# Two gate/up groups per FFN as seven block products instead of eight, in a two-layer decoder trunk on one core

## The chip, the cores and the metric

One NeuronCore of a Trainium2 chip runs the whole kernel in one launch. The metric is the device time of an execution in microseconds (us). TensorE (PE in the profile) multiplies, VectorE (DVE) and ScalarE (ACT) work elementwise, GpSimd (POOL) takes small tasks, SyncE (SP) issues DMAs.

## The reference, cut to what matters

Two layers on 256 tokens of width 1024, in float32. Each layer is FFN, mixer, FFN; four FFNs in all, with an inner width of 2816 = 5 x 512 + 256. Layer 0 mixes by causal pooling, layer 1 by dilated window attention whose keys and values come from the residual stream after layer 0.

```python
def swiglu(h, w_gate, w_up, w_down):
    return (jax.nn.silu(h @ w_gate) * (h @ w_up)) @ w_down

def reference(...):
    for layer in range(DEPTH):
        g = norm_gain[layer]
        f = swiglu(rms_norm(h, g[0]), ffn_w_gate[layer, 0], ffn_w_up[layer, 0], ffn_w_down[layer, 0])
        h = h + 0.5 * rms_norm(f, g[1])
        hm = rms_norm(h, g[2])
        mix = pool_mixer(hm, ...) if layer < N_A_LAYERS else dilated_mixer(hm, ...)
        h = h + rms_norm(mix, g[3])
        f = swiglu(rms_norm(h, g[4]), ffn_w_gate[layer, 1], ffn_w_up[layer, 1], ffn_w_down[layer, 1])
        h = h + 0.5 * rms_norm(f, g[5])
        if layer == N_A_LAYERS - 1:
            k_sh, v_sh = shared_kv(h, kv_norm_gain, w_k, w_v, cos, sin)
    return h
```

## The kernel before

**Precision by parts.** Every float32 operand is split in two float32r parts: `hi`, a cast, and `lo`, the rest. A product is three matmuls: hi·hi, hi·lo, lo·hi. For a weight unit (a tile of 128 x 1024) the load comes from one packed stream `ws`, ScalarE casts (line 92) and VectorE subtracts (line 93); `load_unit` does all three. The raw tile has four buffers (`rawp`), the parts eight (`hlp`, tag `hl`).

**Work order of an FFN.** The normed activations lie transposed in `aT` (two token halves of 128, eight blocks of 128 of the inner dimension). The gate and up columns are taken in five groups of 512 and a last one of 2 x 256. A group of gate, or of up, is four units; `both` goes through them and multiplies each for both token halves, 2 x 2 x 3 = 12 matmuls of 512 columns a unit. `gate` applies SiLU on ScalarE, `up` multiplies on VectorE, `turn` transposes the product on TensorE (four 128 x 128 blocks) and splits it into parts in `h2`. `turn` for group c runs inside the gate half of group c + 1. Gate results lie in the two PSUM banks of `gup`, up results in the four of `accp`. Then 22 units of the down weights follow, one for each block of 128 rows, each with 12 matmuls; the last six (`TAIL`) are first used for token half 0, then for half 1, so that the norms of half 0 run beside matmuls. `Bound` is what lies between two stages: `post` (norm and residual), `norm` (the next stage's), `transposed` (TensorE transposes into PSUM, cast and subtraction into `aT`).

**Order.** The tile framework orders VectorE, ScalarE and TensorE in the FFNs ahead of time by its own planned times, with program order as the priority, and then puts in the waits; on the chip each engine goes through its list in order. In the attention stage the order of TensorE, VectorE and ScalarE is that of the program (`manual_schedule`). SP issues the loads in order, and each waits until its raw buffer is free.

**Other places that the change touches.** `kv_input` norms and transposes the stream for keys and values; it runs in FFN 2 after group 2 (`middle`). In attention `next_q` loads one unit of query weights at a time, `q_turn` copies the transposed queries out of PSUM (line 611), `p_turn` and `values` handle the probabilities, and `o_proj` multiplies by the output weights.

Of the kernel before, what the change touches and what calls it, by code (L numbers as in the profile page):

```python
# [26 lines left out]
NG = 5  # L27
TAIL = 6
WARM = 64
CAST = 1024  # L30
# [17 lines left out]
def trunk_kernel(ctx: ExitStack, tc: tile.TileContext, x, pos, gains, pscale, ws, wq, invf, amask, pmat, icnt, out):  # L48
# [6 lines left out]
    s8p = ctx.enter_context(tc.tile_pool(name="s8p", bufs=6))  # L55
# [25 lines left out]
    unit_no = [0]  # L81
    last = {}

    def load_unit():
        u = unit_no[0]
        unit_no[0] += 1
        raw = rawp.tile([P, 1024], F32, tag="raw", name=f"raw{u}")
        last["dma"] = nc.sync.dma_start(raw, ws[u])
        hl = hlp.tile([P, 2, 1024], F32R, tag="hl", name=f"hl{u}")
        for c in range(0, 1024, CAST):  # L90
            w = slice(c, c + CAST)
            nc.scalar.copy(hl[:, 0, w], raw[:, w])  # L92
            last["dve"] = nc.vector.tensor_sub(hl[:, 1, w], raw[:, w], hl[:, 0, w])  # L93
        return hl

    def load_q_unit(u):
        raw = rawp.tile([P, 1024], F32, tag="raw", name=f"rawq{u}")
        nc.sync.dma_start(raw[:, :768], wq[u])
        hl = hlp.tile([P, 2, 1024], F32R, tag="hl", name=f"hlq{u}")
        nc.scalar.copy(hl[:, 0, :768], raw[:, :768])  # L100
        nc.vector.tensor_sub(hl[:, 1, :768], raw[:, :768], hl[:, 0, :768])  # L101
        return hl
# [4 lines left out]
    def proj_mm(o, aT, i, units, n, nk=8, only=None):  # L107

        per = nk // len(units)
        for q, u in enumerate(units):  # L110
            if only is not None and q != only:
                continue
            for k in range(per):
                kc = q * per + k
                lo, hi = k * n, (k + 1) * n
                t = slice(i * P, (i + 1) * P)
                mm(o, aT[:, 0, kc, t], u[:, 0, lo:hi], kc == 0, False)
                mm(o, aT[:, 0, kc, t], u[:, 1, lo:hi], False, False)
                mm(o, aT[:, 1, kc, t], u[:, 0, lo:hi], False, kc == nk - 1)

    def row_mm(f, l_hi, l_lo, u, first, last):

        mm(f[0], l_hi, u[:, 0, 0:512], first, False)
        mm(f[1], l_hi, u[:, 0, 512:1024], first, False)
        mm(f[0], l_hi, u[:, 1, 0:512], False, False)
        mm(f[1], l_hi, u[:, 1, 512:1024], False, False)
        mm(f[0], l_lo, u[:, 0, 0:512], False, last)
        mm(f[1], l_lo, u[:, 0, 512:1024], False, last)

    def half_mm(f, k, l_hi, l_lo, u, first, last):  # L130
        n = slice(k * 512, (k + 1) * 512)
        mm(f[k], l_hi, u[:, 0, n], first, False)
        mm(f[k], l_hi, u[:, 1, n], False, False)
        mm(f[k], l_lo, u[:, 0, n], False, last)
# [40 lines left out]
    def transposed(i, src, dst, name):  # L175

        for b in range(2):
# [6 lines left out]
            nc.vector.tensor_sub(d[:, 1], tp, d[:, 0])  # L184

# [25 lines left out]
    def ffn(n, aT, boundary, middle=None):  # L211

        h2 = [s8p.tile([P, 2, 4, S], F32R, tag="s8", name=f"h2_{n}_{c}") for c in range(NG + 1)]
        act, prod = {}, {}

        def gate(c, i, g):
            w = g.shape[-1]
            act[c, i] = sc2.tile([P, 512], F32, tag="w2", name=f"s_{n}_{c}{i}")
            nc.scalar.activation(act[c, i][:, :w], g, AF.Silu)

        def up(c, i, u):
            w = u.shape[-1]
            prod[c, i] = sc2.tile([P, 512], F32, tag="w2", name=f"m_{n}_{c}{i}")
# [11 lines left out]
        def both(ps, units, c=None):  # L235

            for q in range(4):
                for i in range(2):
                    proj_mm(ps[i], aT, i, units, 512, only=q)
                if c is not None and q < 2:  # L240
                    turn(c, q)

        units = [load_unit() for _ in range(8 - len(first_units))]
        units, first_units[:] = first_units + units, []
# [11 lines left out]
        for c in range(1, NG):  # L256
            units = [load_unit() for _ in range(4)]
            ps = [gup.tile([P, 512], F32, tag="gu", name=f"g_{n}_{c}{i}") for i in range(2)]
            both(ps, units, c - 1)
            for i in range(2):  # L260
                gate(c, i, ps[i])
            units = [load_unit() for _ in range(4)]
            ps = acc_pair(f"u{n}{c}")
            both(ps, units)
            for i in range(2):
                up(c, i, ps[i])
            if c == 2 and middle is not None:
                middle()
        units = [load_unit() for _ in range(4)]
        ps = [gup.tile([P, 512], F32, tag="gu", name=f"g_{n}_{NG}{i}") for i in range(2)]  # L270
        both(ps, units, NG - 1)
        for i in range(2):
            gate(NG, i, ps[i][:, 0:256])
            up(NG, i, ps[i][:, 256:512])

# [7 lines left out]
        for c in range(NF - TAIL):  # L283
            u = load_unit()
            down(c, 0, u)
            down(c, 1, u)
            if c < 2:
                turn(NG, c, 2)
        tail = [load_unit() for _ in range(TAIL)]
# [12 lines left out]
    class Bound:  # L302


        def __init__(self, n, post_idx, half, pre_idx):
            self.n, self.half, self.idx = n, half, (post_idx, pre_idx)

        def prepare(self):
            self.gpost = load_gain(self.idx[0], "post")
            self.gpre = load_gain(self.idx[1], "pre")  # L310
            self.aT = new_aT(self.n)

# [6 lines left out]
        def third(self, i):  # L319
            transposed(i, self.y, self.aT, self.n)  # L320
# [7 lines left out]
    aT = new_aT("x")  # L328
    with tc.manual_schedule(engines={mybir.EngineType.DVE, mybir.EngineType.Activation}):
        y = norm(0, gpre, "x")  # L330
        first_units += [load_unit()]
# [457 lines left out]
```

## Time and profile before

| | before |
|---|---|
| median of 3 runs | 991.42 us (991.13 to 992.21) |
| profiled execution | 991.82 us, span 990.0 us |
| mean granted TensorE clock | 0.992 |
| PE busy | 966.5 us, 98% |
| DVE busy | 577.4 us, 58% |
| ACT busy | 482.8 us, 49% |
| POOL busy | 55.0 us, 6% |
| DMA read | 178.54 MB |

The span runs from the first to the last instruction of the profiled execution. "Busy" is the time in which an engine works; matmuls are pipelined, so their spacing says more than the duration of one. A row of the groups gives line, engine, operation, result and operands, shapes and count, then the busy time in us and the mean of one in ns, then the idle time just before and what ended it. A row of the chain gives start, duration and what ran. A row of a timeline ends in brackets with the idle time before it and what released it. A row of the stretches gives the bounds, the length, and for PE, weight loads, DVE, ACT and POOL the busy time and count, then the granted clock, the DMA share and GB/s.

### The profile page before, as it was taken

How to read it: one execution, taken by the hardware profiler on the slowest of the kernel's cores; microseconds unless marked ns; L12 is line 12 of the kernel's file. 1: busy time of each engine (PE TensorE's matmuls, PEld its weight loads, DVE VectorE, ACT ScalarE, POOL GpSimd, SP SyncE). 2: the span in 40 equal slices, each digit the busy share in tenths (PEclk: the TensorE clock that was granted, in tenths of full speed). 3: DMA queues.
4: the chain of work that ended last, by engine and by line, in shares of the span. 5: the costliest groups of instructions: out<-in, count | busy, mean ns of one | idle time of the engine just before them, and what ended most of it. 6: DMA issues, size and time to landing. Idle time of an engine off the chain costs nothing.

```text
span 990.0 us, 12277 instructions
## 1 busy us (share of the span) xinstructions
PE 966.5 (98%) x4656; PEld 798.4 (81%) x4656; DVE 577.4 (58%) x740; ACT 482.8 (49%) x665; POOL 55.0 (6%) x50
## 2 busy tenths in 40 slices
PE   7999999999999999999999999999999999999997
PEld 6888888878788888887888888788878678888886
DVE  5665554578765555447666554695366856555542
ACT  5644443366554444347554443554355755444431
POOL 0000000010100000001000000100033500000000
PEclk8999999999999999999999999999999989999999
DMA  6855655656465565535855655475233527556531
GB/s 234 296 178 185 229 187 186 206 192 214 148 214 190 183 229 183 191 128 168 275 181 174 227 187 192 149 234 177 90 98 116 174 83 255 190 190 200 185 128 42
DMA packets 53723, 180.39 MB, mean 182 GB/s; under 512 B 7264, under 2 KB 7264, under 8 KB 53664
## 3 DMA queue, kind: packets, MB, share of 16 engines
q1 hardware_dynamic: 53584, 179.35, 54.9%
q8 instruction: 36, 0.59, 0.2%
q0 software_dynamic: 80, 0.26, 0.1%
q14 instruction: 23, 0.19, 0.1%
HBM read 178.54 MB, written 1.05 MB: 181 GB/s over the span
## 4 chain that ended last, share of the span: by engine, by line
PE 82%; DVE 6%; ACT 4%; issue 4%; POOL 2%; DMA 1%; SPq 0%; POOLq 0%; DVEq 0%; ACTq 0%
PE g L105 22%; PE acc_d L105 21%; PE acc_u L105 19%; PE acc_b L105 7%; PE vp L105 3%; PE kp L105 3%; PE htp L230 2%; DVE hl L93 2%; PE acc_w L105 1%; DVE h L171 1%; PE qp L105 1%; ACT hl L92 1%; ACT p L554 1%; POOL rs_qf L156 1%; DMA gain_pre<-in_gains 1%
## 5 line engine op out<-in xcount | busy, mean ns | idle before, releaser
L93 DVE TENSOR_TENSOR hl<-raw,hl 128x1024 fp32r<-128x1024 f32 x310 | 379.4, 1226 | 295.7 <-ACT hl L92 293.3
L92 ACT CAST hl<-raw 128x1024 fp32r<-128x1024 f32 x310 | 325.2, 1051 | 330.9 <-PE acc_d L105 100.6
L105 PE MATMUL acc_d<-hl,h 128*128 128x512 f32 x1056 | 242.9, 390 | 0.0
L105 PEld LDWEIGHTS acc_d<-hl,h 128*128 128x128 f32 x1056 | 197.4, 188 | 40.6
L105 PE MATMUL g<-hl,aT_m 128*128 128x512 f32 x480 | 116.2, 394 | 0.0
L105 PEld LDWEIGHTS g<-hl,aT_m 128*128 128x128 f32 x480 | 88.6, 188 | 18.0
L105 PE MATMUL acc_u<-hl,aT_m 128*128 128x512 f32 x384 | 88.3, 389 | 0.0
L105 PEld LDWEIGHTS acc_u<-hl,aT_m 128*128 128x128 f32 x384 | 72.1, 188 | 15.0
L105 PE MATMUL acc_u<-hl,aT_f 128*128 128x512 f32 x288 | 67.2, 390 | 0.0
L105 PEld LDWEIGHTS acc_u<-hl,aT_f 128*128 128x128 f32 x288 | 53.8, 188 | 11.4 <-DVE aT_f L184 0.5
L105 PE MATMUL g<-hl,aT_f 128*128 128x512 f32 x240 | 58.8, 396 | 0.0
L105 PE MATMUL g<-hl,aT_x 128*128 128x512 f32 x240 | 58.1, 394 | 0.0
L105 PEld LDWEIGHTS g<-hl,aT_x 128*128 128x128 f32 x240 | 44.3, 188 | 9.0
L105 PEld LDWEIGHTS g<-hl,aT_f 128*128 128x128 f32 x240 | 44.2, 188 | 8.8
L105 PE MATMUL acc_b<-hl,aT_m 128*128 128x512 f32 x192 | 47.5, 408 | 1.2 <-ACT aT_m L183 1.1
L105 PEld LDWEIGHTS acc_b<-hl,aT_m 128*128 128x128 f32 x192 | 37.7, 198 | 9.9 <-ACT aT_m L183 1.3
L105 PE MATMUL acc_u<-hl,aT_x 128*128 128x512 f32 x192 | 44.2, 389 | 0.0
L105 PEld LDWEIGHTS acc_u<-hl,aT_x 128*128 128x128 f32 x192 | 36.0, 188 | 7.5
L105 PE MATMUL qp<-hlq,aT_f 128*128 128x384 f32 x192 | 38.1, 345 | 1.2 <-DVE hlq L101 1.1
L561 POOL TENSOR_SCALAR p<-p,rd 128x512 f32<-128x512 f32 x16 | 30.3, 1905 | 105.8 <-DVE rd L560 99.5
L105 PEld LDWEIGHTS qp<-hlq,aT_f 128*128 128x128 f32 x192 | 32.8, 188 | 3.4 <-DVE hlq L101 2.0
L105 PE MATMUL kp<-hl,aT_hk 128*128 128x512 f32 x144 | 34.6, 394 | 0.0
(156 smaller groups left out, 835.3 us busy)
## 6 DMA issues: line engine op xcount, KB each, us to landing
raw<-in_ws SPq DMA_DIRECT2D x310, 512.0 KB, 3.4
rawq<-in_wq SPq DMA_DIRECT2D x16, 384.0 KB, 3.2
gain_post<-in_gains SPq DMA_DIRECT2D x14, 256.0 KB, 4.9
gain_pre<-in_gains SPq DMA_DIRECT2D x12, 256.0 KB, 5.9
rawpm<-in_pmat SPq DMA_DIRECT2D x2, 512.0 KB, 5.0
out_dram<-h SPq DMA_DIRECT2D x4, 256.0 KB, 2.1
h<-in_x SPq DMA_DIRECT2D x2, 256.0 KB, 3.1
h<-in_x SPq DMA_DIRECT2D x1, 512.0 KB, 8.4
```

The lines of the kernel that those rows point to most:

```text
L92: nc.scalar.copy(hl[:, 0, w], raw[:, w])
L93: last["dve"] = nc.vector.tensor_sub(hl[:, 1, w], raw[:, w], hl[:, 0, w])
L105: nc.tensor.matmul(o, l, r, start=start, stop=stop)
L156: nc.gpsimd.tensor_tensor(rs, ms, nhalf, op=ALU.pow)
L171: nc.vector.scalar_tensor_tensor(h[i][:, c], y[:, c], rs, h[i][:, c], op0=ALU.mult, op1=ALU.add)
L230: nc.tensor.transpose(tp[:, k], prod[c, i][:, k * P : (k + 1) * P], ident)
L554: nc.scalar.activation(p, p, AF.Exp, bias=nm, scale=0.125, accum_out=den)
L561: nc.gpsimd.tensor_scalar_mul(p, p, rd)
```

## The change

Groups 1 and 3 of each FFN are computed with seven block products instead of eight (Winograd's form of Strassen's scheme). The blocks are two token halves by two halves of the inner dimension for the activations, and two halves of the inner dimension by gate and up columns for the weights: x and w are the gate's two halves, y and z the up's. The products are A00·x, A01·w, S0·(x+y), S1·(x+y+z), S3·z, S2·(y+z) and A11·(x+y+z+w), all weight sums formed in place and S0 to S3 are sums of activation blocks, made by the new class `Sums` out of the transposes' PSUM tiles. Results are put together in PSUM by accumulating into the same bank, and by additions on VectorE (c01, c11, p1). Group c + 1 of a pair stays plain, its matmuls set between the products.

Two of a pair's four weight sums are VectorE additions (k = 0, 1), two are accumulating DMAs issued from GpSimd (k = 2, 3, `DMA_SUMS`). The weight stream is laid out in blocks of 128 x 2048, loaded as two DMAs into one raw tile; `form` casts and subtracts a whole block at once into two parts buffers. Raw tiles have three buffers of twice the size, parts six; two more buffers (`xyp`) hold x and y of a pair, and the parts of the first units of some plain groups. The sums of activations take a place in the pool of `aT`, so `kv_input` moves from the middle of FFN 2 to after its last gate/up group (`late`). In attention, query weights are loaded two units at a time, the queries are copied out in three pieces, three buffers instead of four hold the transposed probabilities, and the last output products are set otherwise between the other steps.

```diff
-    rawp = ctx.enter_context(tc.tile_pool(name="rawp", bufs=4))
-    hlp = ctx.enter_context(tc.tile_pool(name="hlp", bufs=8))
+    rawp = ctx.enter_context(tc.tile_pool(name="rawp", bufs=3))
+    xyp = ctx.enter_context(tc.tile_pool(name="xyp", bufs=2))
+    hlp = ctx.enter_context(tc.tile_pool(name="hlp", bufs=6))
...
+    def form(raw):
+
+        hi, lo = [hlp.tile([P, 2, 1024], F32R, tag="hl", name=f"hl_{z}") for z in ("hi", "lo")]
+        nc.scalar.copy(hi, raw)
+        last["dve"] = nc.vector.tensor_sub(lo, raw, hi)
+        return [(hi[:, k], lo[:, k]) for k in range(2)]
...
+        def add_half(self, i, b, tp):
+            a = self.a
+            if (i, b) != (1, 1):
+                a[i, b] = self.tmp(f"{i}{b}")
+                nc.scalar.copy(a[i, b], tp)
+            if (i, b) == (1, 0):
+                s3 = self.tmp("s")
+                nc.vector.tensor_sub(s3, a[0, 0], tp)
+                self.parts(2, s3)
+            if (i, b) == (1, 1):
+                nc.vector.tensor_sub(a[1, 0], tp, a[1, 0])
+                self.parts(0, a[1, 0])
+                nc.vector.scalar_tensor_tensor(a[0, 0], a[0, 0], -1.0, a[1, 0], op0=ALU.mult, op1=ALU.subtract)
+                self.parts(1, a[0, 0])
+                nc.vector.scalar_tensor_tensor(a[0, 1], a[0, 1], -1.0, a[0, 0], op0=ALU.mult, op1=ALU.subtract)
+                self.parts(3, a[0, 1])
+
+        def parts(self, k, src):
+            nc.scalar.copy(self.out[:, k, 0], src)
+            nc.vector.tensor_sub(self.out[:, k, 1], src, self.out[:, k, 0])
...
+        def add(dst, src, k):
+            if k in DMA_SUMS:
+                nc.gpsimd.dma_start(dst, src, accum_op=ALU.add)
+            else:
+                nc.vector.tensor_add(dst, dst, src)
+
+        def pair(c, turns):
+
+            g = [gup.tile([P, 512], F32, tag="gu", name=f"g_{n}_{c}{i}") for i in range(2)]
+            us = load_form()
+            both(g, us + us, (0,))
+            turns[0]()
+            both(g, us + us, (1,))
+            x, y = [load_raw(xyp, "xy") for _ in range(2)]
+            px = bank()
+            product(px, plain(0, 0), form(x), True)
+            p1 = temp("p1")
+            nc.scalar.copy(p1, px)
+            turns[1]()
+            z = load_raw()
+            add(x, y, 0)
+            py = bank()
+            product(py, summed(0), form(x), True)
+            p5 = temp("p5")
+            nc.scalar.copy(p5, py)
+            us = load_form()
+            both(g, us + us, (2, 3))
+            for i in range(2):
+                gate(c + 1, i, g[i])
+            add(x, z, 1)
+            product(px, summed(1), form(x), False)
+            u1 = temp("u1")
+            nc.scalar.copy(u1, px)
+            product(py, summed(3), form(z), False)
+            c01 = temp("c01")
+            nc.vector.scalar_tensor_tensor(c01, py, -1.0, u1, op0=ALU.mult, op1=ALU.subtract)
+            add(y, z, 2)
+            g = [gup.tile([P, 512], F32, tag="gu", name=f"u_{n}_{c}{i}") for i in range(2)]
+            us = load_form()
+            both(g, us + us, (0, 1))
+            product(px, summed(2), form(y), False)
+            c11 = temp("c11")
+            nc.vector.scalar_tensor_tensor(c11, px, -1.0, p5, op0=ALU.mult, op1=ALU.subtract)
+            w = load_raw()
+            pz = bank()
+            product(pz, plain(0, 1), form(w), True)
+            nc.vector.tensor_add(p1, pz, p1)
+            gate(c, 0, p1)
+            up(c, 0, c01)
+            add(x, w, 3)
+            product(px, plain(1, 1), form(x), False)
+            gate(c, 1, px)
+            up(c, 1, c11)
+            us = load_form()
+            both(g, us + us, (2,))
+            turn(c, 0)
+            both(g, us + us, (3,))
+            for i in range(2):
+                up(c + 1, i, g[i])
...
+        pair(1, [lambda: turn(0, 0), lambda: turn(0, 1)])
+        if middle is not None:
+            middle()
...
+        pair(3, [turns12, lambda: turn(2, 1)])
...
+        if late is not None:
+            late()
...
-        nc.scalar.copy(qT[pr // 2][:, pr % 2, :, i * P : (i + 1) * P], tp[:, :3])
+        for g in range(3):
+            nc.scalar.copy(qT[g][:, pr, i * P : (i + 1) * P], tp[:, g])
```

More of the change, by code (lines that the diff above doesn't have):

```diff
@@ L79, in trunk_kernel @@
         nc.tensor.matmul(warm[:, 0:P], zeros, zeros, start=True, stop=True)
-    unit_no = [0]
+    block_no = [0]
     last = {}
[L84 to L94, printed above, removed]
@@ new lines, in load_units, with load_form, load_q_units @@
+    def load_units(n, xy=False):
+        units = []
+        for b in range(n // 2):
+            raw = load_raw()
+            units += [parts(raw, k, xy=xy and b == 0) for k in range(2)]
+        return units
+    def load_form():
+        return form(load_raw())
+    def load_q_units(pr, b):
+        raw = rawp.tile([P, 2, 1024], F32, tag="raw", name=f"rawq{pr}{b}")
+        nc.sync.dma_start(raw[:, :, :768], wq[pr * 2 + b])
+        return [parts(raw, k, 768, pr % 2 == 0 and b == 0) for k in range(2)]
@@ L233, in turn, with both, bank @@
             nc.vector.tensor_sub(d[:, 1], tp[:, :nt], d[:, 0])
[L235 to L237 removed]
+        def both(ps, units, qs=range(4)):
+            for q in qs:
                 for i in range(2):
                     proj_mm(ps[i], aT, i, units, 512, only=q)
[L240 to L244, printed above, removed]
+        def bank():
+            return accp.tile([P, 512], F32, tag="acc", name=f"st{n}")
@@ new lines, in product @@
+        def product(ps, a, units, start):
+            for k in range(4):
+                u = [z[:, (k % 2) * 512 : (k % 2) * 512 + 512] for z in units[k // 2]]
+                for n, (z, v) in enumerate(((0, 0), (0, 1), (1, 0))):
+                    nc.tensor.matmul(
+                        ps,
+                        a(z, k),
+                        u[v],
+                        start=start and k == 0 and n == 0,
+                        stop=k == 3 and n == 2,
+                        skip_group_check=not start,
+                    )
```

242 lines of the change are left out of this document (144 added, 98 removed).

## Prediction

> **What bounds the kernel now.** I read the page's busy shares first, then the chain that ended last inside one gate/up group, then that stretch's busy times, then what the other engines wait for.
>
> ```profile
> PE 966.5 (98%) x4656; PEld 798.4 (81%) x4656; DVE 577.4 (58%) x740; ACT 482.8 (49%) x665; POOL 55.0 (6%) x50
> ...
> PEclk8999999999999999999999999999999989999999
> ...
> q1 hardware_dynamic: 53584, 179.35, 54.9%
> ```
> ```profile
> 296.07 10.88 PE acc_u L105 x48
> 306.95 2.72 PE g L105 x12
> 309.67 0.44 PE htp L230 x4
> 310.11 2.76 PE g L105 x12
> 312.87 0.44 PE htp L230 x4
> 313.30 5.49 PE g L105 x24
> 318.80 10.88 PE acc_u L105 x48
> 329.68 2.72 PE g L105 x12
> ```
> ```profile
> 300.00:345.00 45.00, 45.00 (x208) 37.23 (x207) 24.32 (x24) 20.62 (x24) 0.00 (x0) 1.00 0.55 186
> ```
> ```profile
> ACT hl L92 <- PE acc_d L105: 100.6, 63, 1.7
> ACT hl L92 <- PE acc_u L105: 99.9, 66, 2.0
> ACT hl L92 <- PE g L105: 82.8, 51, 1.7
> ```
> The chain in a group is TensorE alone: 48 matmuls of 512 columns in 10.88 us, 0.2267 us each, and 0.44 us for a block of four transposes. A group (96 matmuls, two blocks) takes 329.68 − 306.95 = 22.73 us. In the stretch 300 to 345 TensorE is busy for all 45.00 us at full clock (the column before the last two), VectorE for 24.32, ScalarE for 20.62. The casts wait for TensorE to give back a parts buffer, 51 to 66 times per kind of user: ScalarE and VectorE are ahead. So a matmul taken out of a group is worth 0.2267 us, as long as VectorE stays ahead.
>
> **What goes.** In each FFN groups 1 and 3 become block products. A plain group is 2 token halves x 2 halves of the inner dimension x 2 matrices = 8 block products of 12 matmuls; seven remain. Two groups in four FFNs: 8 x 12 x 0.2267 = **−21.8 us**, the most that the change can give. Groups 2 and 4 keep their 96 matmuls, spread between the products. A pair of groups is then 84 + 96 = 180 matmuls and four blocks of transposes: 40.8 + 1.8 = 42.6 us where 45.5 stood.
>
> **What VectorE and ScalarE get.** The rows for it:
>
> ```profile
> L93 DVE TENSOR_TENSOR hl<-raw,hl 128x1024 fp32r<-128x1024 f32 x310 | 379.4, 1226 | 295.7 <-ACT hl L92 293.3
> L92 ACT CAST hl<-raw 128x1024 fp32r<-128x1024 f32 x310 | 325.2, 1051 | 330.9 <-PE acc_d L105 100.6 <-PE acc_u L105 99.9 <-PE g L105 82.8
> ...
> L233 DVE TENSOR_TENSOR h<-htp,h 128x512 fp32r<-128x512 f32 x40 | 27.4, 684 | 0.0
> ...
> L232 ACT CAST h<-htp 128x512 fp32r<-128x512 f32 x40 | 23.3, 581 | 0.0
> ...
> L100 ACT CAST hlq<-rawq 128x768 fp32r<-128x768 f32 x16 | 13.4, 836 | 3.1 <-PE vp L105 3.1
> ...
> L194 DVE TENSOR_TENSOR n_f<-h,gain_pre 128x512 f32<-128x512 f32 x12 | 7.7, 686 | 0.0
> ```
> No 2048-wide instruction is in the trace. VectorE: 1226 − 686 ns for 512 more elements gives 1.055 ns each, so 2048 take 1226 + 1080 = 2306 ns; back to back about 2.27. ScalarE: (1051 − 836)/256 = 0.84 ns, so 1.91 us. A pair now needs 11 wide casts and subtractions (seven for products, four for plain halves) where 16 narrow ones stood, two weight sums on VectorE (x+y, then +z), three results (c01, c11, p1+pz), four gate-times-up products and four transposes' parts. VectorE: 11 x 2.27 + 2 x 2.27 + 11 x 0.684 = 37.0 us of the 42.6, **87%** where the stretch above shows 54%. ScalarE: 11 x 1.91 + 11 x 0.58 = 27.4 us, 64%. Neither is the bound by its sum. What counts is the serial order: x is cast, subtracted, summed, cast, subtracted, summed, cast, subtracted, and six parts buffers hold only three forms (8 held eight units, 8 x 12 matmuls = 22 us of work; three forms are 8.2 to 10.9 us).
>
> ```profile
> raw<-in_ws SPq DMA_DIRECT2D x310, 512.0 KB, 3.4
> ...
> qT<-in_amask POOLq DMA_DIRECT2D x1, 256.0 KB, 5.0
> ```
> I walked two pairs of an FFN step by step with these durations, each of the two engines taking the first ready instruction in program order, TensorE in program order. A raw tile is now two loads of 3.4 us, the second issued behind the first; 4.2 us for both is my estimate. The same walk of the old FFN gives 22.65 us per group, against 22.73 in the rows. For the second pair, in us from its first matmul:
>
> ```
> x's first parts ready 0.0; the last pair's two gate-times-up products 0.6
> x+y summed 0.6-2.9; cast 2.9-4.9; subtracted 4.9-7.2        (wanted 9.5)
> two transposes' parts 8.5; next plain half subtracted 10.8   (wanted 12.2)
> a transposes' part 11.5; +z summed 13.7; cast 15.7; subtracted 18.0 (wanted 17.6)
> ```
> TensorE waits 0.43 us for x+y+z there, and 1.34 us in the first pair, where x's loads sit behind group 0's last use of the two chain buffers. At the end of the first pair it waits 1.12 us: the plain `up` results now lie in the two `gup` banks that the next gate half takes at once, while VectorE is inside a 2.27 us subtraction. Waits for products of gate and up ahead of their transposes cost 0.16 and 0.37, and 0.18 us are scattered. Sum 3.60 us per FFN, x4 = **+14.4 us**. A 2.35 us subtraction instead raises it by 1.44 per FFN. So two thirds of the gain go to VectorE's latency.
>
> **The two sums by DMA.** `y+z` is due some 20 us after its operands are there; `x+y+z+w` decides. x+y+z is subtracted at 18.0, and the parts buffers for x+y+z+w come free at the end of the plain half, 28.9. A DMA of 11 us from issue to landing costs nothing; walked on, each further us costs 0.8 to 0.9 us per pair, about 7 us in all.
>
> The bounds: queue 1 moved 179.35 MB in 54.9% of 990 us, 330 GB/s while busy. A block is twice a load: 3.4 + 0.52/0.33 = 5.0 us if it behaves like a load; 4 x 5.0 = 20 us if it scales from POOL's only DMA. That DMA has 5.0 − 0.26/0.33 = 4.2 us beside its bytes; with one pass over 1.05 MB it makes 7.4 us, with two (both operands are read) 10.6. I take 9, between these, since issue from POOL is the nearest row: **0 us**, with little to spare. The Trainium skill, DMA: Bandwidth & Descriptors, section "Anatomy of one DMA — SWDGE (gpsimd) path", gives 2.0 us plus bytes over 436 GB/s; by it an estimate for two passes is 6.8 us and the cost also 0. The row of 256 KB (5.0 us against 2.6) doesn't agree with it.
>
> Against the change speaks what VectorE does to POOL:
>
> ```profile
> 440.30 0.55 POOL L156 TENSOR_TENSOR rs_pf<-ms_pf,nhalf 128x1 f32<-128x1 f32 x1 [171.45 <-DVE ms_pf L154]
> ...
> 444.62 1.22 DVE L93 TENSOR_TENSOR hl<-raw,hl 128x1024 fp32r<-128x1024 f32 x1
> ...
> 444.78 1.46 POOL L156 TENSOR_TENSOR rs_qf<-ms_qf,nhalf 128x1 f32<-128x1 f32 x1 [3.94 <-DVE ms_qf L154]
> ```
> The same one-element instruction takes 0.55 us alone and 1.46 beside a subtraction with two SBUF operands, as if held to its end. A wide subtraction could hold POOL for up to 2.3 us, and it runs 87% of the time. One hold is within the 11 us; a hold at each of many descriptors is not. The Trainium skill, SBUF — State Buffer, section "Who interferes with whom", says that such an instruction contends with GpSimd's SBUF reads, and (as an inference) not with the writing of descriptors; the rows agree with the first, none shows the second.
>
> **The other edits.** The activation sums: eight VectorE and seven ScalarE instructions of 512, some 5.5 and 4.1 us, in four FFNs. They fall beside this part of an FFN's start:
>
> ```profile
> 457.99 1.06 PE L181 MATMUL tp_f<-ident,n_f 128*128 128x128 f32 x8 [0.36 <-DVE n_f L195]
> ...
> 459.96 1.29 DVE L184 TENSOR_TENSOR aT_f<-tp_f,aT_f 128x512 fp32r<-128x512 f32 x2 [2.11 <-ACT aT_f L183]
> ```
> With eight units formed VectorE has room (2.11 us idle before the second row), but the first token half's two copies (1.16 us) stand on ScalarE among the norm's steps, and TensorE waits for these at the boundary (first row). Between 0 and 1.16 I take 0.5, at three boundaries: **+1.5**; the first FFN's sums have group 0 to themselves.
>
> In attention `q_turn` copies three 128x128 pieces instead of one:
>
> ```profile
> L611 ACT COPY qT<-qtp 128x384 f32<-128x384 f32 x8 | 3.8, 478 | 6.5 <-PE qtp L610 6.5
> ...
> L588 ACT CAST oT<-ob 128x128 fp32r<-128x128 f32 x8 | 2.1, 260 | 0.9 <-PE ob L105 0.8
> ```
> 8 x (3 x 260 − 478) = 2.4 us of ScalarE on a stretch that is chained through it; between 0 and 2.4, **+1.2**. There the weights' parts are now made two units at a time, ahead of an `exp` (up to 0.84 us each), three buffers instead of four hold the transposed probabilities, and the last output products are set between the transposes: both signs, −3 to +3, taken as 0. The `kv` transposes move from group 2 to the start of the down product: as many, among matmuls as before, 0; without that cover four blocks of 0.44. Loads stay 512 KB, in the same number; SP's queue holds `x` until the chain buffer is free, with the loads behind it, which the walk contains. Fewer raw buffers in count hold more bytes (24 KB a partition for 16), the pooling matrix is cast in one instruction, and the temporaries need six of their seven buffers: 0. Accumulating into a bank after it was copied makes TensorE wait for c11 only where VectorE is late by more than one product, 2.7 us: 0, in the walk.
>
> **Sum.** −21.8 + 14.4 + 0 + 1.5 + 1.2 = −4.7. The profiled execution took 991.82 us (span 990.0), 0.4 over the median 991.42: 987.1, or 986.7 against the median. I say **986**.
>
> **The rivals.** *VectorE keeps up*: the planner sets the sums and subtractions better than my list and the waits vanish; 991.4 − 21.8 + 2.7 = 972. For it speaks the 87%; against it that three casts of 1.9 us lie inside x's chain. *VectorE falls behind* (the other side): its list is fixed beforehand, and a subtraction standing at the head for its cast holds the next ones. Walked in a fixed order with 3% longer instructions an FFN is 1.4 us slower than now instead of 1.85 faster: 991.4 + 5.7 + 2.7 = 1000. It decides once the waits in a pair pass 2.72 us. *The sums by DMA are late*: at 14 us to landing 986 + 3 x 7 = 1007, at 20 us about 1050; it decides above 11 us plus what is left of the gain, 11.7.
>
> **Chances.** Forecast case 52% (its own range 979 to 992), VectorE keeps up 17%, falls behind 17%, late sums 14%. Changes within 0.2%, 2 us, can't be told from none. Of the forecast case about four fifths lie below 989.4: faster 0.17 + 0.41 = 0.58; same 0.12; slower 0.30. The range 974 to 1003 leaves out the best of the first rival and most of the late sums.
>
> **What would show it.** Right: 96 fewer 512-column matmuls, still near 0.227 us; an FFN's gate/up 1 to 3 us shorter; TensorE idle 1 to 2 us in each pair, ended by the wide subtraction; VectorE near 87% in a pair. Wrong: wide instructions off 2.3 and 1.9 us; `x+y+z+w` landing over 11 us after issue, and TensorE waiting for the last product; an attention stretch changed by more than 3 us; boundaries longer by more than 1 us.

## The result and the profile after

The changed kernel takes 985.6 us (median of 4 runs, 982.64 to 986.07) against 991.41 us: a ratio of 0.9934, with a 95% interval of 0.9913 to 0.9954. The forecast was 986. The number was right by luck: two terms of its sum were wrong, and their errors nearly cancelled. Medians and ratios are over several executions, and a ratio is to the kernel before run beside the version (990.9 us for the versions below). All lengths of stretches are from one profiled execution of each: 991.82 us before (span 990.0), 985.76 us after (span 984.0). One execution of one version below ran at a granted clock of 0.556 for 1580 us; the ratios leave it out.

The page of the changed kernel, busy shares and granted clock:

```profile
span 984.0 us, 12092 instructions
PE 950.4 (97%) x4560; PEld 783.7 (80%) x4560; DVE 684.1 (70%) x771; ACT 542.9 (55%) x693; POOL 62.3 (6%) x66
...
PEclk8999999999999999999999999999999799999999
```

96 matmuls fewer (4656 − 4560), VectorE busy for 107 us more, and a dip in the granted clock at the 32nd slice, deeper than the one that stood at the 33rd before. The groups of its new wide instructions:

```profile
L107 DVE TENSOR_TENSOR hl_lo<-raw,hl_hi 128x2048 fp32r<-128x2048 f32 x48 | 109.4, 2285 | 15.6 <-ACT hl_hi L106 15.5
L106 ACT CAST hl_hi<-raw 128x2048 fp32r<-128x2048 f32 x48 | 91.9, 1914 | 20.8 <-PE st L314 10.6 <-PE g L127 8.0 <-DMA raw<-in_ws 1.3
L107 DVE TENSOR_TENSOR hl_lo<-xy,hl_hi 128x2048 fp32r<-128x2048 f32 x40 | 91.6, 2291 | 48.6 <-ACT hl_hi L106 48.6
```

A wide subtraction takes 2.29 us (2.27 to 2.31 was worked out), a wide cast 1.91 (1.91). Busy times in two stretches of about a pair's length in the second FFN (its first pair starts at 281.1, its second at 324.1):

```profile
284.00:327.00 43.00, 43.00 (x198) 35.38 (x197) 35.71 (x25) 27.01 (x23) 1.75 (x2) 1.00 0.77 245
327.00:371.50 44.50, 43.01 (x196) 34.86 (x195) 35.41 (x28) 28.37 (x26) 1.72 (x2) 1.00 0.78 228
```

VectorE (the third busy time) works 35.7 of 43 us in a pair, 83%; 87% was forecast. TensorE is busy for all of the first 43 us. Where the span went, stretch by stretch ("gate/up" is from a pair's first gate product to the first down product; "attention" from the first query product to the first gate product of the last FFN's pairs):

| stretch | before | after | difference | forecast |
|---|---|---|---|---|
| gate/up of the four FFNs | 102.78, 102.76, 104.69, 102.75 | 98.86, 99.71, 98.90, 99.20 | −16.3 | −7.4 |
| in it, `kv` transposes | 1.9 | 0.8 | −1.1 | 0 |
| the rest of the FFNs, with the other `kv` transposes (1.0 us) | | | +1.1 | 0 |
| start, boundaries, pooling mixer | | | +1.7 | +1.5 |
| keys and values | 69.7 | 70.0 | +0.3 | 0 |
| attention | 111.51 | 118.67 | +7.2 | +1.2 |

Eight of the sixteen `kv` transposes now stand just ahead of the first down product, so still in gate/up as it is measured here; the other eight stand in the down product. Without them gate/up is 15.2 us shorter where 7.4 was forecast, and attention gives back 7.2 us where 1.2 was. The second row is a part of the first; the others add up to −6.0, and the span is 6.0 shorter.

### The profile page after: what moved, and what is told of

Same layout as the page of the kernel before. It is cut to its first block, busy times and chain, and to the rows that moved or that the text cites. A ratio compares the mean times of both kernels' runs of the same rounds, so it can differ in the third digit from the quotient of the medians.

```text
span 984.0 us, 12092 instructions
## 1 busy us (share of the span) xinstructions
PE 950.4 (97%) x4560; PEld 783.7 (80%) x4560; DVE 684.1 (70%) x771; ACT 542.9 (55%) x693; POOL 62.3 (6%) x66
## 4 chain that ended last, share of the span: by engine, by line
PE 74%; DVE 11%; ACT 5%; DMA 4%; issue 3%; POOL 2%; SPq 0%; POOLq 0%; DVEq 0%; ACTq 0%
PE acc_d L127 22%; PE g L127 12%; PE st L314 12%; PE u L127 7%; PE acc_b L127 6%; PE vp L127 3%; DVE hl L100 3%; PE kp L127 3%; DMA xy<-raw 2%; DVE hl_lo L107 2%; PE htp L295 2%; ACT hl L99 2%; PE qp L127 1%; DVE h L193 1%; PE acc_w L127 1%
## 5 line engine op out<-in xcount | busy, mean ns | idle before, releaser
L100 DVE TENSOR_TENSOR hl<-raw,hl 128x1024 fp32r<-128x1024 f32 x182 | 221.0, 1222 | 111.6 <-ACT hl L99 110.5
L99 ACT CAST hl<-raw 128x1024 fp32r<-128x1024 f32 x182 | 189.7, 1051 | 138.3 <-PE acc_d L127 103.3
L107 DVE TENSOR_TENSOR hl_lo<-xy,hl_hi 128x2048 fp32r<-128x2048 f32 x40 | 91.6, 2291 | 48.6 <-ACT hl_hi L106 48.6
L107 DVE TENSOR_TENSOR hl_lo<-raw,hl_hi 128x2048 fp32r<-128x2048 f32 x48 | 109.4, 2285 | 15.6 <-ACT hl_hi L106 15.5
L106 ACT CAST hl_hi<-xy 128x2048 fp32r<-128x2048 f32 x40 | 76.5, 1913 | 64.0 <-DVE xy L333 29.7
L106 ACT CAST hl_hi<-raw 128x2048 fp32r<-128x2048 f32 x48 | 91.9, 1914 | 20.8 <-PE st L314 10.6
L127 PEld LDWEIGHTS acc_b<-hl,aT_m 128*128 128x128 f32 x192 | 35.7, 188 | 8.3 <-ACT aT_m L205 0.8
L127 PE MATMUL g<-hl_hi,aT_m 128*128 128x512 f32 x128 | 41.9, 393 | 0.0
L127 PE MATMUL u<-hl_hi,aT_m 128*128 128x512 f32 x128 | 41.8, 393 | 0.0
L314 PE MATMUL st<-hl_hi,S_m 128*128 128x512 f32 x128 | 41.8, 393 | 0.0
L127 PE MATMUL qp<-hl,aT_f 128*128 128x384 f32 x192 | 38.9, 354 | 0.0
```

What stands on the lines that cost most here:

```text
L99: nc.scalar.copy(hl[:, 0, :n], raw[:, k, :n])
L100: last["dve"] = nc.vector.tensor_sub(hl[:, 1, :n], raw[:, k, :n], hl[:, 0, :n])
L106: nc.scalar.copy(hi, raw)
L107: last["dve"] = nc.vector.tensor_sub(lo, raw, hi)
L127: nc.tensor.matmul(o, l, r, start=start, stop=stop)
L314: nc.tensor.matmul(ps, a(z, k), u[v], start=start and k == 0 and n == 0, stop=k == 3 and n == 2, skip_group_check=not start,)
```

## The experiments: attention

Four edits of the change lie in attention; the forecast gave them 1.2 us, all of it for copies. The timeline of the changed kernel where TensorE waits first (each row: start, duration, what ran, and in brackets the idle time before it with its releaser; rows of other instructions left out):

```profile
714.62 2.26 DVE L100 TENSOR_TENSOR hl<-rawq,hl 128x768 fp32r<-128x768 f32 x2 [1.05 <-ACT hl L99]
...
718.39 0.68 DVE L710 CUSTOM_DVE_ANT_0 p<-sc,qT 128x512 f32<-128x512 f32 x1
...
719.31 0.72 ACT L714 ACTIVATE p<-p,nm 128x512 f32<-128x512 f32 x1 [3.98 <-DVE nm L712]
...
720.48 3.11 POOL L721 TENSOR_SCALAR p<-p,rd 128x512 f32<-128x512 f32 x2 [4.40 <-DVE rd L720]
...
720.82 1.05 ACT L737 COPY qT<-ptp 128x512 f32<-128x512 f32 x2
...
721.43 2.46 PE L127 MATMUL ob<-qT,kv 128*64 128x128 f32 x16 [2.22 <-ACT qT L737]
```

Two query units' parts, made one behind the other, hold VectorE from 714.62; the masked maximum (line 710) comes late, ScalarE's `exp` has sat idle for 3.98 us, the copy of the transposed probabilities comes at 720.82, and TensorE has waited 2.22 us. Then the clock falls. Five-microsecond stretches of the changed kernel (bounds, length, busy times, then, third from the end, the granted clock):

```profile
720.00:725.00 5.00, 3.57 (x20) 3.04 (x21) 0.72 (x5) 3.44 (x12) 3.11 (x2) 0.66 0.18 71
...
755.00:760.00 5.00, 1.43 (x9) 0.88 (x7) 3.84 (x12) 2.07 (x6) 0.00 (x0) 0.89 0.88 302
760.00:765.00 5.00, 4.75 (x23) 4.22 (x24) 1.47 (x5) 3.38 (x9) 3.11 (x2) 0.50 0.30 119
...
775.00:780.00 5.00, 3.73 (x26) 3.12 (x28) 1.50 (x6) 1.27 (x3) 0.34 (x1) 0.60 0.01 3
780.00:785.00 5.00, 5.00 (x28) 4.27 (x25) 0.78 (x4) 3.27 (x10) 3.11 (x2) 0.72 0.00 0
```

The kernel before has one such place:

```profile
790.00:795.00 5.00, 1.90 (x12) 1.23 (x10) 4.25 (x8) 3.87 (x9) 2.01 (x2) 0.90 0.55 188
795.00:800.00 5.00, 4.85 (x11) 3.81 (x12) 4.56 (x9) 1.94 (x7) 1.46 (x1) 0.50 0.05 21
```

The idle times before TensorE's rows in attention add up to 11.7 us after and 7.9 before. So of the 7.2 us, 3.8 are more waiting. The other 3.3 (118.67 − 11.69 against 111.51 − 7.86) go with the lower clock: it is at 0.50 for 17.1 us of the stretch after and for 6.8 before, so the same matmuls take longer. The experiments ask which edit makes them. "Bunch" blames the query units made in twos, "tail" the new places of the last output products, "copies" the three query copies and the three buffers.

**Query units one at a time, on the changed kernel.** Per pair of units one load stays, and the parts are made at the step where the kernel before made them:

```diff
-        if k % 2 == 0:
-            units.extend(load_q_units(pr + 1, k // 2) if pr < 3 else load_units(2))
+        if k % 2 == 0:
+            half_raw[0] = ...        # the load of both
+        units.append(parts(half_raw[0], k % 2, ...))
```

> The changed kernel (985.6 us) with one edit: in attention the query weights are again split into parts one unit at a time, each at the place where the old kernel did it; the loads stay as they are. The attention stretch, from the first query product to the first gate matmul of the last FFN, went from 111.5 to 118.7 us with the change. Theory 'bunch' (two casts and two subtractions in a row hold up the masked maximum and the exp behind them, TensorE then waits for the probabilities and its clock falls): the stretch comes back to 112 to 114.5, the time to 979.5 to 982. Rival 'tail' (the new order of the last output products costs it): 985 to 986.5. Rival 'copies' (three query copies, three probability buffers): 985 to 986.5.

Measured: 981.42 us, ratio 0.9904 (0.9891 to 0.9917); attention 115.5 us, 3.1 less, where "bunch" wanted 112 to 114.5. The wait of 2.22 us at 721 is gone. Others stay: the timeline has

```profile
759.14 1.75 PE L127 MATMUL ob<-qT,kv 128*64 128x128 f32 x16 [3.53 <-ACT qT L737]
```

and 1.77 us before a transpose at 772.51. TensorE's idle time in the stretch falls by 1.0 us only, to 10.7, since waits of 0.30, 0.55 and 1.03 us stand there instead; but the clock is at 0.50 for 10.2 us in place of 17.1. Bunching costs, and it is not all.

**The old order at attention's end, on the changed kernel** (the block from `o_proj(0, (0,))` to `go.third(0)` as in the kernel before).

> The changed kernel with one edit: the output products, score products and transposes after the last head pair stand in the order of the old kernel. 'bunch': 984.5 to 986.5, no clear difference. 'tail': the stretch loses 4 us or more, 979 to 982. 'copies': 984.5 to 986.5.

Measured: 980.47 us, ratio 0.9898 (0.9885 to 0.9912); attention 113.5 us, 5.2 less, as "tail" wanted; 9.7 us are idle, and the clock is at 0.50 for 6.8. Here the early wait stays, at 722.28 with 2.23 us, and of the waits of 1.33, 0.89 and 0.88 us between 773 and 779 one of 0.88 is left. Each theory is right about its own place, and neither alone: what a theory said of the other's run (no change) is wrong for both.

**Both, with the queries copied in two pieces.**

```diff
-        for g in range(3):
-            nc.scalar.copy(qT[g][:, pr, i * P : (i + 1) * P], tp[:, g])
+        two = qx[0].rearrange("p g (r s) -> p g r s", r=4)
+        nc.scalar.copy(two[:, :, pr, i * P : (i + 1) * P], tp[:, 0:2])
+        nc.scalar.copy(qT[2][:, pr, i * P : (i + 1) * P], tp[:, 2])
```

> The changed kernel with the two edits above and with the queries copied out in two pieces instead of three (the three probability buffers stay). If the 7.2 us of the stretch lie in these three edits together: 978 to 980. 'bunch' alone: the same as the first run within 1 us. If 'copies' counts, 1 to 2 us under the sum of the first two runs' gains. If the three buffers are the cause: 984 to 986.

Measured: 978.13 us, ratio 0.9873 (0.9859 to 0.9887); attention 111.8 us, close to the kernel before (111.5), although three buffers for the transposed probabilities remain. The clock has one shallow dip left:

```profile
755.00:760.00 5.00, 2.99 (x19) 2.42 (x20) 2.20 (x7) 4.31 (x10) 0.14 (x1) 0.79 0.65 210
760.00:765.00 5.00, 5.00 (x30) 4.26 (x30) 3.89 (x9) 0.23 (x2) 3.05 (x2) 0.87 0.57 211
```

The nearly equal lengths are not the same waits. The kernel before waits 2.18 and 1.07 us at the end of the stretch. Here 0.39 us of those are left, and a wait that it doesn't have stands ahead of an `ob` product. The chain to that product goes through the load of an output weight, for which ScalarE, in its fixed order, stands still:

```profile
751.17 1.05 ACT L99 CAST hl<-raw 128x1024 fp32r<-128x1024 f32 x1 [3.29 <-DMA raw<-in_ws]
...
756.95 2.02 PE L127 MATMUL ob<-qT,kv 128*64 128x128 f32 x16 [3.25 <-ACT qT L737]
```

It remains with both edits. The load is issued when a raw buffer comes free; the fewer and larger raw buffers were 0 in the forecast, and no run here takes them back.

**Both, the copies left in three pieces.**

> The changed kernel with single query loads and the old order at attention's end, the queries' copies left in three pieces (whole forms). My prediction's term for the copies in three pieces in place of one was 1.2 us, between 0 and 2.4. Theory 'copies on the path': against the version with two pieces, 978.1 us, this one is 0.6 to 1.2 us slower, and from the first query product to the last FFN's first gate product it takes 112.4 to 113 us (111.8 there, 111.5 in the kernel before). Rival 'copies covered': the same to 0.4 us, 977.7 to 978.5.

Measured: 978.86 us, ratio 0.9883 (0.9863 to 0.9904), attention 112.72 us, 0.93 more than with two pieces. The stretch lies in the range of "copies on the path", but doesn't show it. The clock is at 0.50 for 6.8 us in this profile and for 3.4 in the other, and 3.4 us more at half clock are worth up to 1.7. Versions below with two pieces and the same attention code take from 111.75 to 113.15 us, and the four executions of the one with two pieces take 977.01 (the profiled one) to 979.71 us, at mean granted clocks of 0.997 to 0.992. By the times, too, the two versions can't be told apart: the price of the copies stays open.

**Bunching alone, on the kernel before** (two query units loaded and split at every second step).

> The kernel before (991.4 us) with one part of the change alone: query weights loaded and split two units at a time (at the first and third place instead of at all four). 'bunch': 995 to 997.5, with TensorE waiting for probabilities or their copies in the attention stretch. 'tail' and 'copies': 990.5 to 992.

Measured: 992.92 us, ratio 1.0019 (1.001 to 1.0028); attention 112.5 us, 0.95 more. Neither range is hit: the time is 2.0 us over the kernel before beside it (990.93), less than "bunch" wanted and more than the others. Up to the last FFN's first product it loses 3.2 us (89.31 against 86.07), and 2.3 come back there: it does not have the half clock of 795 to 800, and its own dip, 0.76 from 780 to 785, is shallower. Whether that is the edit's doing or the execution's, one profile of each can't tell. So a bunched unit has no fixed price: what it costs depends on the waits around it.

## The experiments: the pairs

The four FFNs' gate/up would be 97.33 us each if all 24 matmuls' time were gained, and 98.12 in the third, with eight `kv` transposes (0.79 us) in it. The changed kernel is above that by 6.6 us in all; TensorE's rows there have waits of 1.02, 1.49, 0.20 and 1.02 us. The first, in a timeline with VectorE beside it:

```profile
97.91 2.29 DVE L107 TENSOR_TENSOR hl_lo<-xy,hl_hi 128x2048 fp32r<-128x2048 f32 x1 [1.61 <-ACT hl_hi L106]
...
98.85 0.39 PE L314 MATMUL st<-hl_hi,S_x 128*128 128x512 f32 x1
...
100.26 0.50 PE L314 MATMUL st<-hl_lo,S_x 128*128 128x512 f32 x1 [1.02 <-DVE hl_lo L107]
100.60 0.62 PE L314 MATMUL st<-hl_hi,S_x 128*128 128x512 f32 x2
```

This is the forecast's wait for `x+y+z`: the product's first matmul has `hi`, the second wants `lo`, and VectorE is inside the wide subtraction. It stands in this pair alone, the one in which VectorE also makes the angle tables, with instructions of about 0.2 us between the links of `x`'s chain; the other three FFNs have no angle tables and no wait for `x+y+z`. A wait costs more than its idle time, which counts from the modelled end of the matmul before: the starts above are 1.41 us apart where 0.23 is usual, and the next ones 0.34, so this wait costs 1.29 us. Counted so, the eight waits of these four parts cost 5.8 of the 6.6 us.

In the second pair of the second FFN the chain goes through the last DMA sum (start, duration, what):

```profile
337.23 4.03 DMA raw<-in_ws
...
341.82 12.20 DMA xy<-raw
...
354.13 1.92 ACT hl_hi L106
...
358.96 2.20 DVE hl_lo L107
...
878.78 11.65 DMA xy<-raw
```

The sum is issued at 341.82, once the load of `w` has landed, and lands 12.20 us later; the last row is the same sum of the last FFN. TensorE waits 0.89 and 0.44 us at the last product behind them. In the last FFN:

```profile
892.47 2.29 DVE L107 TENSOR_TENSOR hl_lo<-xy,hl_hi 128x2048 fp32r<-128x2048 f32 x1 [4.15 <-ACT hl_hi L106]
894.68 0.68 DVE L371 SCALAR_TENSOR_TENSOR c<-st,p 128x512 f32<-128x512 f32 x1
...
895.51 0.47 PE L314 MATMUL st<-hl_hi,aT_m 128*128 128x512 f32 x1 [0.44 <-DVE c L371]
```

The product doesn't wait for the sum's parts, but for `c11` (line 371), which has to be read out of the bank that the product adds to. In VectorE's list `c11` stands behind the subtraction of the late sum, and VectorE sits idle for 4.15 us ahead of that subtraction. The runs that follow are made from the version with the three edits in attention (978.13 us, ratio 0.9873, called the base), so that less in attention hides them; its four gate/up parts take 98.87, 99.89, 98.90 and 98.95 us.

**The last sum on VectorE** (`DMA_SUMS = (2,)`).

> The version with single query loads, the old order at attention's end and copies in two pieces (978.1 us), and x+y+z+w summed by VectorE instead of by a DMA. Theory 'landing': what is left of TensorE's waits in the pairs (3.66 us in the four FFNs of that version) hangs in good part on the last sum's 12 us from issue to landing; VectorE has room for 2.28 us more per pair. Then the waits at the last product of the second pairs (1.04 and 0.16 us) go and nothing else appears: 976 to 978. Rival 'VectorE', the rate of my walk: 1.44 us per FFN for 0.08 us on each of 26 instructions, so 0.69 us for each us put on VectorE. 2.28 us in eight pairs cost 12.6 us: 991, and each pair is about 1.6 us longer.

Measured: 976.84 us, ratio 0.9861 (0.9847 to 0.9874); gate/up 100.22, 98.20, 98.94, 98.08. In the second and the last FFN the waits at the last product are gone; in the first FFN, where VectorE also makes the angle tables, a second wait of 1.06 us appears. VectorE's 2.28 us more per pair don't cost the 12.6 us of my rate. So "landing" is right about the waits that go, and wrong in that another appears; its gain of 1.3 us is within the two intervals.

**Both DMA sums on VectorE** (`DMA_SUMS = ()`).

> As the run before, with both y+z and x+y+z+w summed by VectorE: no accumulating DMA is left, and loads have the queues for themselves. VectorE in a pair goes from some 36 to some 40.5 of 43 us. Theory 'landing': VectorE still has room, loads of x and y land in 3.4 to 5 us instead of 6.4: 975 to 979. Rival 'VectorE': twice 12.6 us, 1003; half of it or more, 988 to 1003, would say that the two DMAs are what keeps VectorE off the path.

Measured: 983.88 us, ratio 0.9929 (0.9916 to 0.9941), 5.7 us over the base; gate/up 100.79, 99.71, 100.56, 99.74, together 4.2 more. Neither theory hits. A first pair has VectorE at 38.9 of 43 us and TensorE 0.6 idle:

```profile
467.98:510.98 43.00, 42.38 (x193) 34.65 (x192) 38.90 (x25) 26.04 (x21) 0.00 (x0) 1.00 0.58 200
```

In a stretch of the same kind the base has 35.7 us and the version with one sum more 37.8, both without idle time of TensorE. So VectorE begins to show between one and two sums more, at about 90% of a pair. Where it shows is one place in the order: the addition of `y+z` stands directly ahead of the subtraction that the plain `up` half wants.

```profile
301.89 2.29 DVE L333 TENSOR_TENSOR xy<-xy,raw 128x2048 f32<-128x2048 f32 x1
304.09 2.28 DVE L107 TENSOR_TENSOR hl_lo<-raw,hl_hi 128x2048 fp32r<-128x2048 f32 x1
...
306.43 0.50 PE L127 MATMUL u<-hl_lo,aT_m 128*128 128x512 f32 x1 [0.58 <-DVE hl_lo L107]
```

Whether the load or this place is the cause, no run separates.

**`x+y+z` by DMA too** (`DMA_SUMS = (1, 2, 3)`).

> x+y+z is summed by a DMA too; only x+y stays on VectorE, which has 2.28 us less per pair. Theory 'landing': x+y+z stands in x's serial chain; its subtraction ended at 18.0 us of the pair in my walk where 17.6 was wanted, so 8.2 us of landing in place of 2.3 us of addition show almost whole, some 5 us per pair, of which TensorE's other work covers none: 978 + 8 x 5 = 1018, at the least 995. Rival 'VectorE': its load is what sets the waits, so 2.28 us less of it gains 3 us or leaves the time: 975 to 979.

Measured: 1022.67 us, ratio 1.0318 (1.0304 to 1.0332). "Landing" is right, with a pair 5.9 us longer where 5 was expected. The chain of a first pair, in order of time:

```profile
299.21 10.37 DMA xy<-raw
...
309.60 1.91 ACT hl_hi L106
...
311.53 2.30 DVE hl_lo L107
...
313.88 7.08 PE st L314 x23
```

23 matmuls take 7.08 us behind this wait, where 5.21 is the usual (23 x 0.2267). TensorE had waited 2.66 and 1.82 us just before, and the granted clock is 0.50 for the first of them, which the estimate had left out:

```profile
313.90:317.20 3.30, 3.30 (x8) 2.62 (x9) 3.30 (x2) 2.18 (x2) 0.86 (x1) 0.50 0.59 119
```

As a DMA, the sum that stands in `x`'s serial chain costs some 6 us a pair.

**Forms in two halves** (casts and subtractions 1024 wide).

```diff
-        nc.scalar.copy(hi, raw)
-        last["dve"] = nc.vector.tensor_sub(lo, raw, hi)
+        for k in range(2):
+            nc.scalar.copy(hi[:, k], raw[:, k])
+            last["dve"] = nc.vector.tensor_sub(lo[:, k], raw[:, k], hi[:, k])
```

> The forms' casts and subtractions in two halves of 1024 (1.23 us each on VectorE, 1.05 on ScalarE) instead of one of 2048: VectorE has 11 x 0.17 = 1.8 us more in a pair, but nothing waits for more than 1.2 us behind an instruction. Theory 'grain', a part of my prediction (TensorE waits while VectorE is inside a 2.27 us subtraction): the waits of 1.02 us at the first FFN's second pair and of 0.4 us at the plain up half halve: 976 to 978. Rival 'VectorE load' at 0.69 us per us: 978 + 8 x 1.3 = 988. If neither shows, both are covered: 978.

Measured: 974.68 us, ratio 0.9836 (0.9823 to 0.985); gate/up 97.48, 97.56, 98.19, 97.49. No row of TensorE in them shows a wait, and 0.6 us are left of the base's 6.5 above the full gain. More VectorE work, less time: "grain" is right, beyond what it promised.

**Only the subtractions in halves**, and **only the casts in halves.**

> The forms' subtractions alone in two halves of 1024; the casts stay 2048 wide. With casts and subtractions in halves the gate/up parts of the four FFNs took 97.48, 97.56, 98.19 and 97.49 us (98.87, 99.89, 98.90, 98.95 with whole ones; 97.33 would be the full gain). Theory 'subtraction': what counts is that the first half's lo part is there 1.07 us earlier and VectorE is given to others between. Then this run has the same gate/up parts to 0.3 us each and 974 to 976. Rival 'cast': the first half's subtraction waits for the whole cast, 1.91 us, in place of 1.05; then a good part of the waits stays: gate/up 98.3 to 99, 976.5 to 978.

Measured: 974.03 us, ratio 0.9834 (0.9819 to 0.9848); gate/up 97.87, 98.01, 98.10, 97.66, with 0.25 us of waits in the four together. The first two are 0.4 us above the run with both in halves, a little more than the 0.3 that "subtraction" allowed.

> The forms' casts alone in two halves; one subtraction of 2048. Theory 'subtraction': nothing is gained, since the subtraction waits for both halves, which take 2.10 us in place of 1.91: 978 to 979, gate/up as with whole forms or 0.2 us longer. Rival 'cast': TensorE's first products need hi only, so hi being there earlier gains what the halves of both gained, 974.5 to 976.

Measured: 977.45 us, ratio 0.9865 (0.9848 to 0.9882); gate/up 98.66, 99.54, 98.88, 98.81, in all 0.7 less than the base. The subtraction decides. With it in halves (row below: 1.22 us each, in sum 0.15 us more per form than one of 2.29) the first unit's `lo` is there 1.07 us sooner:

```profile
L108 DVE TENSOR_TENSOR hl_lo<-xy,hl_hi 128x1024 fp32r<-128x1024 f32 x80 | 96.3, 1220 | 46.2 <-ACT hl_hi L106 46.2
```

Other instructions can also run on VectorE between the halves; which of the two wins the time, no run separates.

This version, with single query units, the old end of attention, two query copies and subtractions of 1024, beats both kernels: 974.03 us against 990.86 for the kernel before beside it, 17 us or 1.7%. Its attention takes 113.2 us, 1.4 more than the base's, with the same code there. The rows say where: it is the wait for the output weight's load.

```profile
749.02 2.12 ACT L99 CAST hl<-raw 128x1024 fp32r<-128x1024 f32 x2 [4.40 <-DMA raw<-in_ws]
...
754.80 2.46 PE L128 MATMUL ob<-qT,kv 128*64 128x128 f32 x16 [4.36 <-ACT qT L738]
```

The load lands 5.7 us after its issue, where the base's took 4.6; TensorE waits 1.1 us longer, and the clock is then at 0.50 for 6.8 us instead of 3.4. Why the load is slower here isn't shown.

## Why the number was right, and which steps were not

**The matmuls: right.** 96 fewer, and TensorE is at full clock and without a wait in most of a pair.

**TensorE's waits in the pairs: the term was mis-sized, 14.4 forecast, 6.6 measured.** Of my list, 1.34 us for `x+y+z` in each first pair did not appear at all. The 1.12 us for `up` results in the `gup` banks at a first pair's end did not either; there is a wait of that kind, 0.40 and 0.36 us, at the end of two second pairs. The 0.43 us in each second pair stood as 1.02 us in the first FFN, beside the angle tables, which the walk did not have, and nowhere else. Three second pairs wait 0.20 to 0.22 us for a plain half, and 0.89 and 0.44 us stand behind late sums. The sign "idle 1 to 2 us in each pair" failed: the four first pairs have no wait. The mechanism was as stated, the wide subtraction's length, and the runs with halves showed it: of the base's 6.5 us above the full gain 1.5 stay with the subtractions in halves, and 0.6 with the casts too. What failed was the walk, in which each engine took the first ready instruction of the program: the planner's order has fewer of these waits, by which of its choices was not tested. The idle times of the eight waits are 3.7 us, and counted by the starts of matmuls, as the walk counts, they cost 5.8. The rate read from the walk, 0.69 us for each us of VectorE, was false: one sum more per pair cost nothing on balance, two cost 4.2 us in all.

**The sums by DMA: 0 was forecast, and two of the last sums cost a little.** The landing took 6.9 to 12.2 us, median 8.1, where I took 9:

```profile
xy<-raw POOLq DMA_DIRECT2D x16, 1024.0 KB, 8.1
...
raw<-in_ws SPq DMA_DIRECT2D x278, 512.0 KB, 4.8
```

Eleven us were to cost nothing, and each further one 0.8 to 0.9 us. Of the eight last sums (7.9 to 12.2 us) three took longer: those of 12.20 and 11.65 us had waits of 0.89 and 0.44 us behind them (1.0 and 0.55 by that rate), one of 11.4 us in the first FFN had none, and with the sum on VectorE no wait is left there. What the product waits for is `c11`, a term that the forecast had at 0 unless VectorE is late by 2.7 us. With casts and subtractions in halves last sums of 11.4 to 12.2 us have no wait behind them. Loads took 4.8 us instead of 3.4; by the chain it is `w`'s load that the sum's issue waits for, at 17.7 us of the pair, where the walk had 18.0. The estimate from the Trainium skill, DMA: Bandwidth & Descriptors, section "Anatomy of one DMA — SWDGE (gpsimd) path", was 6.8 us for two passes; it agrees with the shortest of the sixteen, not with the median.

**Boundaries: about right.** The two outside attention are 0.5 and 0.7 us longer, where 0.5 each was forecast; the third lies in the attention stretch, and the other 0.5 of the +1.7 is the start, which varies from 37.0 to 39.9 us among the versions. The rows are like these of the changed kernel, where 0.36 us stood before the transposes and nothing before the product:

```profile
443.42 8.52 PE L127 MATMUL acc_b<-hl,aT_f 128*128 128x512 f32 x36 [0.28 <-ACT aT_f L205]
...
452.74 1.06 PE L203 MATMUL tp_f<-ident,n_f 128*128 128x128 f32 x8 [0.80 <-DVE n_f L256]
```

No run took the activation sums away, so that this is theirs is argued, not shown. The `kv` move cost nothing, as forecast.

**Attention: the step that failed.** "Both signs, −3 to +3, taken as 0" for the bunched units, the three buffers and the moved output products was +6, outside the range given; what the 1.2 for the copies should have been is open. The step costed the edits by instructions, which hardly changed, and not by the order in which engines reach them. In the loop over the head pairs the program fixes VectorE's and ScalarE's order; behind the loop, at attention's end, it fixes TensorE's alone, unlike what is said further up. In the loop a 2.26 us block of subtractions stands ahead of a maximum, and TensorE waits 2.22 us behind `exp`, the scaling on POOL and a copy. It had no term for the clock either, which goes with 3.3 of the 7.2 us. The prediction's own sign for it, an attention stretch changed by more than 3 us, came true.

**The rivals.** The pairs came out about halfway between the forecast case (14.4 us of waits) and "VectorE keeps up" (none): the waits didn't vanish, but with casts and subtractions in halves they nearly do. "Falls behind" and "late sums" didn't happen as a whole. But the former's mechanism, a subtraction at the head of VectorE's list that holds the next instructions, is what the late sums' waits show, and the run with `x+y+z` by DMA shows the latter's price.

## What to carry to other kernels

Where one engine feeds TensorE, cost a wide instruction by when its first useful half is out and by what stands behind it, not by its throughput: splitting it cost 0.15 us of VectorE each and won 4 us here. In a stage whose order is fixed by hand, cost a moved step by what is queued behind it on its engine, and follow that to TensorE. And a right total is no proof of a sum: compare the stretches, since here 8 us too many in the pairs hid 6 too few in attention.

## What the hardware showed that I had not expected

TensorE's granted clock can fall to a half after short waits. Microsecond stretches of the changed kernel around the first wait in attention:

```profile
719.00:720.00 1.00, 0.21 (x2) 0.00 (x0) 0.93 (x6) 0.69 (x2) 0.00 (x0) 1.00 0.94 353
...
721.00:722.00 1.00, 0.57 (x4) 0.37 (x6) 0.11 (x1) 1.00 (x4) 1.00 (x1) 0.70 0.04 15
722.00:723.00 1.00, 1.00 (x11) 1.00 (x12) 0.00 (x0) 0.37 (x3) 1.00 (x2) 0.50 0.00 0
723.00:724.00 1.00, 1.00 (x9) 0.67 (x6) 0.00 (x0) 0.07 (x1) 0.59 (x1) 0.50 0.00 0
724.00:725.00 1.00, 1.00 (x4) 1.00 (x5) 0.33 (x2) 1.00 (x3) 0.00 (x0) 0.59 0.00 0
725.00:726.00 1.00, 1.00 (x8) 1.00 (x7) 1.00 (x2) 0.66 (x1) 0.00 (x0) 1.00 0.00 0
```

An idle time of 2.2 us, from 719.2 to 721.4, is followed by 3.4 us at half clock (0.30, 0.50, 0.50 and 0.41 us lost in the four rows): the wait costs up to 1.7 us more than itself. A wait of 1.27 us, at 740, left the clock alone, and so did one of 2.07 us in the run that bunches the kernel before (764.78 to 766.85), so the length of a wait alone doesn't decide. The Trainium skill, TensorE: Matmul & The Clock Gate, section "What's actually happening", knows two rates, full and half, and a return after about 3.4 us of work; the 0.50 and the 3.4 us agree. It puts the fall behind an idle window of about 3.4 us, and here 2.2 us of idleness was enough.

A third accumulating DMA per pair raised the median landing only from 8.2 to 8.6 us. With `y+z` alone by DMA it is 7.0, but the base's `y+z` sums, two DMAs to a pair, have 7.1 as well: it is the last sums, 8.2 to 12.2 us there, that take long, and why is not shown.
